# A two-layer hybrid decoder trunk on one core: state space input moved to another queue in longer pieces, and the end of the mixers reordered

## Chip, core and metric

The kernel runs on one core of one Trainium2 chip. The metric is the device time of one execution in microseconds (us), and times of several runs are given as their median. The engines are called as the profile calls them: PE is TensorE's matmul, PEld its weight load, DVE is VectorE, ACT is ScalarE, POOL is GpSimd, and SP is SyncE, which only starts transfers here.

## What is computed

Two decoder layers over 256 tokens of width 1024, all in float32. Each layer multiplies its input by one wide matrix, feeds three token mixers (an RWKV-7 time mix, multi-head latent attention, and a diagonal state space model called S5), gates and sums their outputs, normalizes, and ends with a SwiGLU network:

```python
for l in range(DEPTH):                       # DEPTH = 2
    p = x @ w_in[l]
    y_a = rwkv7_time_mix(p[..., :o_mla], ...)
    y_b = mla_branch(p[..., o_mla:o_s5], cos, sin, ...)
    y_c = s5_branch(p[..., o_s5:o_gate], ...)
    gates = sigmoid(p[..., o_gate:].reshape(bsz, t, 3, D_MODEL) + gate_b[l])
    merged = gates[..., 0, :] * y_a + gates[..., 1, :] * y_b + gates[..., 2, :] * y_c
    x = layer_norm(ALPHA * x + merged @ w_out[l], ln1_g[l], ln1_b[l])
    h = silu(x @ ffn_w1[l]) * (x @ ffn_w3[l])
    x = layer_norm(ALPHA * x + h @ ffn_w2[l], ln2_g[l], ln2_b[l])
```

## The kernel before

**Weights.** All large weights lie in DRAM as a list of 512 KB tiles (128 partitions by 1024 floats) in the order of use, 138 to a layer. For each tile SP starts one load into one of three `raw` buffers (line 160), ACT casts it to the high part `whi` (line 161), and DVE, in part POOL, computes the low part `wlo` as the remainder (lines 171 and 173). The high and low parts have four buffers each. A product with a weight is three matmuls: high by high, high by low, low by high (lines 206 to 208); a tile takes 24 of them, 8 on each line. `w_next` (line 194) hands out the next tile and, before that, lists loads until four tiles are queued, so a load that another function lists directly falls three tiles behind the tile in hand.

**Order of the work.** `ORDER1` and `ORDER2` list the units of a layer, and the loops over them (line 1283 for the second) call one function for a token. Each engine works its own instructions strictly in its order, and that order is fixed when the program is built: it follows the list, but a later unit's instructions are placed into a gap where an earlier one is expected to wait. So the units that need nothing but weights fill PE while the mixers' long chains run. In `ORDER2` these fillers are `h` (two tiles, a gate of the time mix), `o` (three tiles: a gate and the output product of the attention) and `l` (two tiles, S5's output). `v1` is the last solve of the time mix, `n1` and `y1` are the two halves of its group norm, `f0` to `f3` are its output products (one tile each, `branch0`, line 1274), which need `y1`'s result.

**Early weights.** `X` (`free`, line 1262) closes the buffers of the mixers and opens a pool on their place; `E0` to `E3` (`ffn_early`, `w_early`, line 175) each load a tile of the feed forward network through a `raw` buffer and cast it to `eh` and `el` in that pool. So the cast waits until the last instruction of `y1` is done, and the `raw` buffer is held from the load until then.

**State space input.** `s5_in` (line 692) copies the projected input out of PSUM to `u` on ACT (line 113 by way of `cp`), and eight transfers of 64 KB spread it over partitions into `U2` (line 702): SP starts them in layer 0, POOL in layer 1. Each is 32 partitions by four pieces of 512 bytes. `s5_tile` (line 724) multiplies `U2` by the tables (line 733). The profile shows these tensors as `u` and `U`.

**End of the mixers.** `norm` (line 1101) takes the square (ACT), the sum and the scale (DVE, with a power on POOL, line 240), and in its second half transposes `yT` on PE (line 1116). `out_half` (line 834) ends each output product with two DVE operations (lines 841 and 842), and the first of them frees its PSUM buffer. There are three `mm` buffers of PSUM. `token_major` (line 497) is the product with `w_out`: the first four row tiles are taken as they come, for both halves of the tokens, then four rows together; its accumulators are the three `mm` buffers and one more, and its rows 2i and 2i+1 are what `f`i wrote.

Of the kernel before, what the change touches and what calls it, by code (L numbers as in the profile page):

```python
# [19 lines left out]
NF = 22  # L20
# [9 lines left out]
ORDER2 = [  # L30
    "U K Q p0 V a0 b0 s0 a1 b1 p1 s1 i0 G0 a2 p2 l1 s2 p3 a3 l0 j0 v0 n0 s3 l2 b2 b3 l3 o3 i1 j1 v1 y0 C n1 h0 y1 h3 o1 h2 o0 X h1 f3 o2 E0 E1 E2 f0 E3 f1 f2",
    "U K Q p0 V a0 s0 a1 b0 p1 s1 i0 p2 l0 a2 b1 s2 l2 p3 b2 j0 v0 a3 s3 i1 n0 y0 l1 b3 j1 l3 v1 C h0 n1 y1 o3 X o2 E0 o0 o1 h2 E1 f0 h1 f1 h3 f3 f2 E2 E3",
]
# [40 lines left out]

PART = {"b": "a", "y": "n", "j": "i", "w": "t", "K": "U", "Q": "U", "V": "U"}


# [9 lines left out]
def trunk(ctx: ExitStack, tc: tile.TileContext, xT, xtok, ws, spA, spB, spC, sp5, lnv, cst, out, dbg=None,  # L87
# [113 lines left out]
    def inst(i):  # L201
        return getattr(i, "ins", i)

    def mm3(ps, w, x, first, last):
        (wh, wl), (xh, xl) = w, x
        PE.matmul(ps, lhsT=wh, rhs=xh, start=first, stop=False)  # L206
        PE.matmul(ps, lhsT=wh, rhs=xl, start=False, stop=False)  # L207
        PE.matmul(ps, lhsT=wl, rhs=xh, start=False, stop=last)  # L208

# [286 lines left out]

    def token_major(a, nk, ln, last, q, l, at):

        nonlocal x_dram
        lg = q.tile([128, D], F32, tag="lg", name="lg")  # L500
        lb = q.tile([128, D], F32, tag="lb", name="lb")
# [3 lines left out]
        def run(w, k, b, ns=(0, 1)):  # L505
            t = slice(128 * b, 128 * b + 128)
            for n in ns:
                s = slice(512 * n, 512 * n + 512)
                ah, al = a[0][:, k, t], a[1][:, k, t]
                PE.matmul(acc[b][n], lhsT=ah, rhs=w[0][:, s], start=(k == 0), stop=False)  # L510
                PE.matmul(acc[b][n], lhsT=ah, rhs=w[1][:, s], start=False, stop=False)  # L511
                PE.matmul(acc[b][n], lhsT=al, rhs=w[0][:, s], start=False, stop=(k == nk - 1))  # L512
# [36 lines left out]
    for l in range(layers):  # L549
# [138 lines left out]
        with tc.tile_pool(name=f"s5p{l}", bufs=1, side=P) as q:  # L688
            u = q.tile([128, 4, 2, 128], F32, tag="u", name="u")
            U2 = q.tile([128, 8, 128], F32, tag="U2", name="U2")  # L690

            def s5_in(fp):
                mark("s5proj")
                ps = proj_pair(X)
                for i in range(2):
                    cp(5, out=u[:, 2 * fp:2 * fp + 2, i, :], in_=ps.rearrange("p (f c i) -> p f i c", f=2, i=2)[:, :, i, :])
                if fp == 0:
                    return
                for j in range(4):
                    for i in range(2):  # L700
                        r = 64 * (j % 2) + 32 * i
                        (G if l else SY).dma_start(out=U2[r:r + 32, j // 2::2, :], in_=u[32 * j:32 * j + 32, :, i, :])

# [20 lines left out]
            def s5_tile(F):  # L724
# [4 lines left out]
                for pp in range(2):  # L729
                    ps = mxps("a")  # L730
                    for qq in range(2):
                        for ri in range(2):
                            PE.matmul(ps[:, 256 * qq + 128 * ri:256 * qq + 128 * ri + 128],  # L733
                                      lhsT=bl[64 * pp:64 * pp + 64, 2 * F + qq, ri, :],
                                      rhs=U2[64 * pp:64 * pp + 64, 2 * F + qq, :], start=True, stop=True)
                    ps4 = ps.rearrange("p (q r t) -> p q r t", q=2, r=2)
# [26 lines left out]
                for j in range(4):  # L763
                    qq, pp = j // 2, j % 2
                    r = slice(64 * pp, 64 * pp + 32)
                    PE.matmul(ps[32 * j:32 * j + 32, 0:128], lhsT=k0[r, 2 * F + qq, :], rhs=U2[r, 2 * F + qq, :],
                              start=True, stop=False, skip_group_check=True)
                for par in range(2):
                    for i, (ci, which, ri) in enumerate(((0, 0, 0), (0, 1, 1), (1, 1, 0), (1, 0, 1))):
                        for j in range(4):  # L770
# [6 lines left out]
                            else:  # L777
                                PE.matmul(ps[32 * j:32 * j + 32, 128:256], lhsT=lt, rhs=src, start=(i == 0),
                                          stop=(i == 3), skip_group_check=True)
                V.scalar_tensor_tensor(out=yc5[:, F, :].rearrange("p (c i) -> p i c", i=2), in0=u[:, F], scalar=A("d", F),  # L780
                                       in1=v2(ps[:, 0:256], 2), op0=ALU.mult, op1=ALU.add)
# [66 lines left out]
        if True:  # L848
# [252 lines left out]
            def norm(g):  # L1101
# [12 lines left out]
                ps = mxps("c")  # L1114
                for i in range(4):
                    PE.transpose(ps[:, 256 * (i % 2) + 128 * (i // 2):256 * (i % 2) + 128 * (i // 2) + 128],
                                 yT[:, 2 * i:2 * i + 2].rearrange("p h n -> p (h n)"), ident)
                yc = t1("BK", (128, 512))
# [170 lines left out]
        with tc.tile_pool(name=f"mg{l}", bufs=1, side=P) as q:  # L1289
            mark("wout")  # L1290
            token_major(gate0[1], 8, 0, False, q, l, [])
        gstack.close()
# [4 lines left out]
        with tc.tile_pool(name=f"ff{l}", bufs=1, side=O) as q:  # L1297
# [54 lines left out]
            with tc.tile_pool(name=f"mh{l}", bufs=1, side=P) as q2:  # L1352
                token_major((hh, hl), NF, 2, l == layers - 1, q2, l, [9, 10, 11, 12])

# [42 lines left out]
def _pack(inp):  # L1397
# [25 lines left out]
    for l in range(nl):  # L1423
# [30 lines left out]
        ws += [piece[t] for t in (ORDER1[l] + " " + ORDER2[l]).split() if t in piece]  # L1454
        ws.append(rows(g["w_out"][l]))
        w1, w3 = g["ffn_w1"][l], g["ffn_w3"][l]
# [71 lines left out]
```

## Time and profile before

| | us |
|---|---|
| median of 3 runs | 1059.97 (1058.11 to 1062.94) |
| the profiled execution | 1062.76 |
| its span, first to last instruction | 1061.0 |
| PE busy | 1012.5 (95%) |
| DVE busy | 785.4 (74%) |
| ACT busy | 485.4 (46%) |
| POOL busy | 238.8 (23%) |
| mean granted TensorE clock | 0.976 of full speed |

PE is busy nearly all of the span, so its idle stretches are short and can be listed one by one. The granted clock has two levels, 1.2 and 2.4 GHz, which the profile writes as 0.5 and 1.0. Times inside the trace are counted from the span's start.

### The profile page before, as it was taken

The page shows a single profiled execution, that of the slowest core. Times are in us where ns is not written, and L with a number is a line of the kernel's source. Part 1 is how long each engine was busy: PE and PEld are TensorE (multiplying, and loading weights), DVE is VectorE, ACT ScalarE, POOL GpSimd, SP SyncE. Part 2 cuts the span into 40 slices and gives each one's busy share as a digit, 9 for nine tenths or more (in the row PEclk, how much of TensorE's full clock was granted, in tenths as well). Part 3 has the DMA queues.
Part 4 walks back from the last instruction along what each step waited for, and adds up shares of the span by engine and source line. Part 5 has one row for each costly group of instructions (what it writes and reads, how often), then busy time and mean ns, then how long its engine had stood idle before and what let it go on. Part 6 is the DMA issues. An engine that isn't in the chain of part 4 may idle for free.

```text
span 1061.0 us, 21306 instructions
## 1 busy us (share of the span) xinstructions
PE 1012.5 (95%) x8584; PEld 910.9 (86%) x8584; DVE 785.4 (74%) x1546; ACT 485.4 (46%) x813; POOL 238.8 (23%) x270
## 2 busy tenths in 40 slices
PE   8799799999999999999998999999998899999997
PEld 7799688887897999998788989788888779999885
DVE  7969988976578778874474898898846776766546
ACT  5554467544343344443344336865343424444431
POOL 2980032200000599500022103121002420000000
PEclk9989889999999999999997999999999999999998
DMA  8543141231475655557645325223234745555572
GB/s 282 156 160 120 60 145 45 81 121 61 162 266 160 212 184 168 171 191 269 202 141 157 101 80 196 94 80 101 85 116 149 249 152 172 189 183 179 182 274 80
DMA packets 46787, 163.87 MB, mean 154 GB/s; under 512 B 5728, under 2 KB 7264, under 8 KB 46048
## 3 DMA queue, kind: packets, MB, share of 16 engines
q1 hardware_dynamic: 46144, 161.46, 46.1%
q8 instruction: 67, 1.10, 0.4%
q0 software_dynamic: 256, 0.52, 0.2%
q10 hardware_dynamic: 288, 0.52, 0.1%
q14 instruction: 32, 0.26, 0.1%
HBM read 156.72 MB, written 4.19 MB: 152 GB/s over the span
## 4 chain that ended last, share of the span: by engine, by line
PE 71%; DVE 15%; DMA 6%; ACT 4%; issue 2%; POOL 1%; SPq 0%; DVEq 0%; ACTq 0%; POOLq 0%
PE mm L208 14%; PE mm L206 14%; PE mm L207 14%; DMA raw<-in_ws 5%; PE mm L511 3%; PE mm L512 3%; PE mm L510 3%; DVE wlo L171 2%; ACT whi L161 2%; DVE z L752 2%; PE pa L960 1%; PE pa L733 1%; PE pa L1210 1%; PE pc L511 1%; PE pc L512 1%
## 5 line engine op out<-in xcount | busy, mean ns | idle before, releaser
L171 DVE TENSOR_TENSOR wlo<-raw,whi 128x1024 fp32r<-128x1024 f32 (+2 forms) x265 | 331.6, 1256 | 171.2 <-ACT whi L161 162.7
L161 ACT CAST whi<-raw 128x1024 fp32r<-128x1024 f32 (+2 forms) x267 | 277.6, 1043 | 366.3 <-PE mm L207 227.0
L206 PE MATMUL mm<-xh,whi 128*128 128x256 f32 x1312 | 378.4, 288 | 7.6 <-ACT whi L161 7.1
L208 PE MATMUL mm<-xh,wlo 128*128 128x256 f32 x1312 | 376.5, 287 | 2.5 <-DVE wlo L171 2.3
L207 PE MATMUL mm<-xl,whi 128*128 128x256 f32 x1312 | 376.3, 287 | 0.4 <-DVE xl L262 0.4
L206 PEld LDWEIGHTS mm<-xh,whi 128*128 128x128 f32 x1312 | 250.2, 191 | 13.0 <-ACT whi L161 7.5
L208 PEld LDWEIGHTS mm<-xh,wlo 128*128 128x128 f32 x1312 | 250.8, 191 | 5.8 <-DVE wlo L171 3.3
L207 PEld LDWEIGHTS mm<-xl,whi 128*128 128x128 f32 x1312 | 250.8, 191 | 3.5 <-issue 1.2
L240 POOL TENSOR_TENSOR rs<-rs,mhalf 128x1 f32<-128x1 f32 x8 | 7.8, 971 | 329.8 <-DVE rs L238 329.8
L206 PE MATMUL mm<-yh,whi 128*128 128x256 f32 x256 | 74.6, 291 | 0.3 <-ACT yh L113 0.2
L207 PE MATMUL mm<-yl,whi 128*128 128x256 f32 x256 | 74.1, 289 | 0.0
L208 PE MATMUL mm<-yh,wlo 128*128 128x256 f32 x256 | 74.0, 289 | 0.0
L511 PE MATMUL mm<-wlo,hh 128*128 128x512 f32 x132 | 52.0, 394 | 0.0
L510 PE MATMUL mm<-whi,hh 128*128 128x512 f32 x132 | 51.6, 394 | 0.0
L512 PE MATMUL mm<-whi,hl 128*128 128x512 f32 x132 | 51.5, 393 | 0.0
L206 PEld LDWEIGHTS mm<-yh,whi 128*128 128x128 f32 x256 | 48.5, 190 | 2.2 <-ACT qa L113 0.9
L208 PEld LDWEIGHTS mm<-yh,wlo 128*128 128x128 f32 x256 | 48.5, 190 | 2.0 <-issue 1.4
L207 PEld LDWEIGHTS mm<-yl,whi 128*128 128x128 f32 x256 | 48.5, 190 | 1.2 <-issue 0.6
L173 POOL TENSOR_TENSOR wlo<-raw,whi 128x384 fp32r<-128x384 f32 (+2 forms) x24 | 27.6, 1153 | 85.3 <-ACT whi L161 84.8
L967 POOL TENSOR_SCALAR_AFFINE_SELECT Mk<-Mk 64x512 f32<-64x512 f32 x32 | 26.5, 829 | 46.3 <-ACT Mk L113 45.0
L511 PEld LDWEIGHTS mm<-wlo,hh 128*128 128x128 f32 x132 | 24.8, 188 | 6.0 <-DVE wlo L171 0.6
L510 PEld LDWEIGHTS mm<-whi,hh 128*128 128x128 f32 x132 | 24.8, 188 | 5.9 <-DVE th L1306 0.5
(492 smaller groups left out, 1731.2 us busy)
## 6 DMA issues: line engine op xcount, KB each, us to landing
raw<-in_ws SPq DMA_DIRECT2D x267, 512.0 KB, 3.5
raw<-in_ws SPq DMA_DIRECT2D x8, 416.0 KB, 3.5
xd<-xk SPq DMA_DIRECT2D x3, 1024.0 KB, 5.7
lg<-in_lnv SPq DMA_DIRECT2D x4, 512.0 KB, 4.8
lb<-in_lnv SPq DMA_DIRECT2D x4, 512.0 KB, 5.2
xk<-xd SPq DMA_DIRECT2D x4, 512.0 KB, 5.2
pc<-in_spC SPq DMA_DIRECT2D x2, 768.0 KB, 5.3
pb<-in_spB SPq DMA_DIRECT2D x2, 512.0 KB, 5.1
```

Of the source, the lines that this page charges most:

```text
L161: S.copy(out=hi[:, s], in_=raw[:, s])
L171: V.tensor_tensor(out=lo[:, 0:m], in0=raw[:, 0:m], in1=hi[:, 0:m].bitcast(F32), op=ALU.subtract)
L173: G.tensor_tensor(out=lo[:, m:w], in0=raw[:, m:w], in1=hi[:, m:w].bitcast(F32), op=ALU.subtract)
L206: PE.matmul(ps, lhsT=wh, rhs=xh, start=first, stop=False)
L207: PE.matmul(ps, lhsT=wh, rhs=xl, start=False, stop=False)
L208: PE.matmul(ps, lhsT=wl, rhs=xh, start=False, stop=last)
L510: PE.matmul(acc[b][n], lhsT=ah, rhs=w[0][:, s], start=(k == 0), stop=False)
L511: PE.matmul(acc[b][n], lhsT=ah, rhs=w[1][:, s], start=False, stop=False)
L512: PE.matmul(acc[b][n], lhsT=al, rhs=w[0][:, s], start=False, stop=(k == nk - 1))
L733: PE.matmul(ps[:, 256 * qq + 128 * ri:256 * qq + 128 * ri + 128], lhsT=bl[64 * pp:64 * pp + 64, 2 * F + qq, ri, :], rhs=U2[64 * pp:64 * pp ...
L752: V.tensor_tensor_scan(out=z[:, pp, qq, ri], data0=bc(m2[:, j:j + 1], [128, 128]), data1=z[:, pp, qq, ri], initial=0.0, op0=ALU.mult, op1= ...
L967: G.affine_select(out=Mk[r, h], in_=Mk[r, h], pattern=[[0, 4], [1, 2], [1, 64]], compare_op=ALU.is_ge, fill=0.0, base=-1, channel_multipli ...
```

## The change

The state space input changes its layout so that each partition's share of a transfer is one piece of 2 KB, and ACT starts the eight transfers in both layers. The transposes of the group norm get an order edge: they may not stand before the last product of three (line 208) that was listed ahead of them. `ORDER2` is changed: in layer 0 `h3` is listed ahead of `y1`; in layer 1 the end is rewritten. The rows of `w_out` are packed and used in the order of the `f` units, so that the rows of the last `f` come last.

```diff
 ORDER2 = [
-    "... y0 C n1 h0 y1 h3 o1 h2 o0 X h1 f3 o2 E0 E1 E2 f0 E3 f1 f2",
-    "... l3 v1 C h0 n1 y1 o3 X o2 E0 o0 o1 h2 E1 f0 h1 f1 h3 f3 f2 E2 E3",
+    "... y0 C n1 h0 h3 y1 o1 h2 o0 X h1 f3 o2 E0 E1 E2 f0 E3 f1 f2",
+    "... l3 v1 C n1 h0 o3 y1 X E0 o0 E1 h3 f3 E2 f0 o2 h2 E3 f2 o1 h1 f1",
 ]
+def wout_rows(l):
+    return [k for t in ORDER2[l].split() if t[0] == "f" for k in (2 * int(t[1]), 2 * int(t[1]) + 1)]
...
+    def behind():
+
+        return tc.issue_after(inst(state["mm"]))
+
     def mm3(ps, w, x, first, last):
...
-        PE.matmul(ps, lhsT=wl, rhs=xh, start=False, stop=last)
+        state["mm"] = PE.matmul(ps, lhsT=wl, rhs=xh, start=False, stop=last)
...
-    def token_major(a, nk, ln, last, q, l, at):
+    def token_major(a, rows, ln, last, q, l, at):
...
-                ah, al = a[0][:, k, t], a[1][:, k, t]
+                ah, al = a[0][:, rows[k], t], a[1][:, rows[k], t]
...
-            u = q.tile([128, 4, 2, 128], F32, tag="u", name="u")
-            U2 = q.tile([128, 8, 128], F32, tag="U2", name="U2")
+            u = q.tile([128, 2, 4, 128], F32, tag="u", name="u")
+            U2 = q.tile([128, 2, 4, 128], F32, tag="U2", name="U2")
...
-                        (G if l else SY).dma_start(out=U2[r:r + 32, j // 2::2, :], in_=u[32 * j:32 * j + 32, :, i, :])
+                        S.dma_start(out=U2[r:r + 32, j // 2], in_=u[32 * j:32 * j + 32, i])
...
-                for i in range(4):
-                    PE.transpose(ps[:, 256 * (i % 2) + 128 * (i // 2):256 * (i % 2) + 128 * (i // 2) + 128],
-                                 yT[:, 2 * i:2 * i + 2].rearrange("p h n -> p (h n)"), ident)
+                with behind():
+                    for i in range(4):
+                        PE.transpose(ps[:, 256 * (i % 2) + 128 * (i // 2):256 * (i % 2) + 128 * (i // 2) + 128],
+                                     yT[:, 2 * i:2 * i + 2].rearrange("p h n -> p (h n)"), ident)
...
-            token_major(gate0[1], 8, 0, False, q, l, [])
+            token_major(gate0[1], wout_rows(l), 0, False, q, l, [])
...
-        ws.append(rows(g["w_out"][l]))
+        ws.append(rows(g["w_out"][l])[wout_rows(l)])
```

The operations on the copies of `u` and on `U2` index the new layout and are otherwise the same. The packing of the weight list follows `ORDER2`.

## Rows read from the trace of the kernel before

**Rows 1.** The page, busy time of each engine over the span.

```profile
PE 1012.5 (95%) x8584; PEld 910.9 (86%) x8584; DVE 785.4 (74%) x1546; ACT 485.4 (46%) x813; POOL 238.8 (23%) x270
```

**Rows 2.** PE's waits: what it waited for, us in total, times, longest us.

```profile
PE mm L206 <- ACT whi L161: 7.1, 2, 5.6
PE pc L1116 <- DVE yT L1111: 4.8, 2, 3.1
```

**Rows 3.** Timelines, layer 1's state space input: start, us, instruction [idle before <- releaser].

```profile
563.81 0.64 ACT L113 COPY u<-mm 128x256 f32<-128x256 f32 x2
564.49 4.58 POOL L702 DMA_DIRECT2D U<-u  x8 [5.11 <-ACT u L113]
565.23 1.05 ACT L161 CAST whi<-raw 128x1024 fp32r<-128x1024 f32 x1 [0.78 <-DMA raw<-in_ws]
...
571.13 2.15 PE L733 MATMUL pa<-U,bl 64*128 64x128 f32 x8 [3.77 <-DMA U<-u]
573.21 0.58 PE L206 MATMUL mm<-xh,whi 128*128 128x256 f32 x1
```

**Rows 4.** Transfers of the page: queue, count, KB each, median us from issue to landing.

```profile
U<-u SPq DMA_DIRECT2D x8, 64.0 KB, 3.0
...
U<-u POOLq DMA_DIRECT2D x8, 64.0 KB, 5.8
```

**Rows 5.** Issue of a transfer: line 702 (ns min/median/max), and ACT's timeline at the start.

```profile
L702 SPq DMA_DIRECT2D U<-u x8: 585/600/1354, 33.5 to 38.8; - x8
...
0.81 0.89 ACTq L251 DMA_DIRECT2D xr<-in_xT  x2
```

**Rows 6.** Windows: stretch, us, busy us (count) of PE, PEld, DVE, ACT, POOL, then PEclk.

```profile
48.30:58.60 10.30, 6.34 (x28) 6.04 (x29) 6.49 (x6) 6.23 (x11) 10.22 (x8) 0.50 0.36 112
...
570.60:584.20 13.60, 12.99 (x53) 11.82 (x54) 6.21 (x13) 1.56 (x2) 0.00 (x0) 0.50 0.28 71
...
806.10:809.50 3.40, 3.20 (x15) 3.21 (x16) 1.75 (x4) 0.00 (x0) 0.00 (x0) 0.50 0.40 135
...
840.20:843.60 3.40, 3.09 (x7) 2.48 (x8) 3.40 (x5) 1.74 (x2) 0.00 (x0) 0.50 0.77 242
```

**Rows 7.** Timelines of ACT and PE, layer 0's first stage.

```profile
48.76 1.33 ACT L418 ACTIVATE cd<-pb,c 128x512 f32<-128x512 f32 x2 [4.86 <-DVE pb L408]
50.00 0.45 ACT L600 ACTIVATE kr__236<-mm,dv 128x256 f32<-128x256 f32 x1
50.36 1.03 ACT L161 CAST whi<-raw 128x1024 fp32r<-128x1024 f32 x1
...
51.45 0.58 PE L206 MATMUL mm<-xh,whi 128*128 128x256 f32 x1 [5.62 <-ACT whi L161]
```

**Rows 8.** Windows with line 208 alone, layer 1: us, PE busy (count), PEld busy (count), PEclk.

```profile
767.50:811.30 43.80, 18.73 (x62) 12.04 (x61) 0.96 0.35 116
811.30:834.40 23.10, 18.08 (x65) 12.06 (x65) 1.00 0.77 259
```

**Rows 9.** Weight loads of 759 to 812.9, `whi` casts of 768 to 812.9, ACT's next casts.

```profile
L160 SPq DMA_DIRECT2D raw<-in_ws x11: 327/328/328, 759.4 to 807.0; - x11
...
L161 ACT CAST whi<-raw x9: 1041/1047/1048, 768.9 to 812.3; 128x1024 fp32r<-128x1024 f32 x9
...
813.23 1.99 ACT L161 CAST eh<-raw 128x1024 fp32r<-128x1024 f32 x2
```

**Rows 10.** Timelines of DVE and PE around the group norm, layer 1 and layer 0.

```profile
797.55 0.69 DVE L1096 TENSOR_REDUCE ssm<-pb 128x8 f32<-128x512 f32 x1 [0.94 <-PE pb L1092]
...
806.30 1.11 PE L1116 MATMUL pc<-c,yT 128*128 128x128 f32 x4 [3.13 <-DVE yT L1111]
...
812.26 0.69 DVE L1129 TENSOR_TENSOR yl<-BK,yh 128x512 fp32r<-128x512 f32 x1
...
281.12 0.66 PE L1116 MATMUL pc<-c,yT 128*128 128x128 f32 x4 [1.63 <-DVE yT L1111]
```

**Rows 11.** Timelines of ACT, DVE and PE at the start of layer 1's `w_out`.

```profile
836.55 1.04 ACT L161 CAST whi<-raw 128x1024 fp32r<-128x1024 f32 x1 [2.01 <-DMA raw<-in_ws]
...
839.78 0.68 DVE L841 SCALAR_TENSOR_TENSOR gate<-gate,mm 128x512 f32<-128x512 f32 x1
...
840.51 0.80 PE L510 MATMUL mm<-whi,msh 128*128 128x512 f32 x1 [4.23 <-DVE gate L841]
```

More of the change, by code (lines that the diff above doesn't have):

```diff
@@ L30 @@
 ORDER2 = [
-    "U K Q p0 V a0 b0 s0 a1 b1 p1 s1 i0 G0 a2 p2 l1 s2 p3 a3 l0 j0 v0 n0 s3 l2 b2 b3 l3 o3 i1 j1 v1 y0 C n1 h0 y1 h3 o1 h2 o0 X h1 f3 o2 E0 E1 E2 f0 E3 f1 f2",
-    "U K Q p0 V a0 s0 a1 b0 p1 s1 i0 p2 l0 a2 b1 s2 l2 p3 b2 j0 v0 a3 s3 i1 n0 y0 l1 b3 j1 l3 v1 C h0 n1 y1 o3 X o2 E0 o0 o1 h2 E1 f0 h1 f1 h3 f3 f2 E2 E3",
+    "U K Q p0 V a0 b0 s0 a1 b1 p1 s1 i0 G0 a2 p2 l1 s2 p3 a3 l0 j0 v0 n0 s3 l2 b2 b3 l3 o3 i1 j1 v1 y0 C n1 h0 h3 y1 o1 h2 o0 X h1 f3 o2 E0 E1 E2 f0 E3 f1 f2",
+    "U K Q p0 V a0 s0 a1 b0 p1 s1 i0 p2 l0 a2 b1 s2 l2 p3 b2 j0 v0 a3 s3 i1 n0 y0 l1 b3 j1 l3 v1 C n1 h0 o3 y1 X E0 o0 E1 h3 f3 E2 f0 o2 h2 E3 f2 o1 h1 f1",
 ]
@@ L495, in layer_norm @@
         yield
-    def token_major(a, nk, ln, last, q, l, at):
+    def token_major(a, rows, ln, last, q, l, at):
         nonlocal x_dram
+        nk = len(rows)
         lg = q.tile([128, D], F32, tag="lg", name="lg")
@@ L695, in s5_in @@
                 for i in range(2):
-                    cp(5, out=u[:, 2 * fp:2 * fp + 2, i, :], in_=ps.rearrange("p (f c i) -> p f i c", f=2, i=2)[:, :, i, :])
+                    cp(5, out=u[:, i, 2 * fp:2 * fp + 2, :], in_=ps.rearrange("p (f c i) -> p f i c", f=2, i=2)[:, :, i, :])
                 if fp == 0:
@@ L734, in s5_tile @@
                                       lhsT=bl[64 * pp:64 * pp + 64, 2 * F + qq, ri, :],
-                                      rhs=U2[64 * pp:64 * pp + 64, 2 * F + qq, :], start=True, stop=True)
+                                      rhs=U2[64 * pp:64 * pp + 64, qq, F, :], start=True, stop=True)
                     ps4 = ps.rearrange("p (q r t) -> p q r t", q=2, r=2)
@@ L765, in s5_tile @@
                     r = slice(64 * pp, 64 * pp + 32)
-                    PE.matmul(ps[32 * j:32 * j + 32, 0:128], lhsT=k0[r, 2 * F + qq, :], rhs=U2[r, 2 * F + qq, :],
+                    PE.matmul(ps[32 * j:32 * j + 32, 0:128], lhsT=k0[r, 2 * F + qq, :], rhs=U2[r, qq, F, :],
                               start=True, stop=False, skip_group_check=True)
@@ L779, in s5_tile @@
                                           stop=(i == 3), skip_group_check=True)
-                V.scalar_tensor_tensor(out=yc5[:, F, :].rearrange("p (c i) -> p i c", i=2), in0=u[:, F], scalar=A("d", F),
+                V.scalar_tensor_tensor(out=yc5[:, F, :].rearrange("p (c i) -> p i c", i=2), in0=u[:, :, F], scalar=A("d", F),
                                        in1=v2(ps[:, 0:256], 2), op0=ALU.mult, op1=ALU.add)
@@ L1352, in trunk @@
             with tc.tile_pool(name=f"mh{l}", bufs=1, side=P) as q2:
-                token_major((hh, hl), NF, 2, l == layers - 1, q2, l, [9, 10, 11, 12])
+                token_major((hh, hl), range(NF), 2, l == layers - 1, q2, l, [9, 10, 11, 12])
 def _constants():
```

## The prediction

> **What bounds the kernel now.** I read the page first: PE is busy 95% of the span [rows 1], so only PE's idle time and stretches at half clock can be won. Next came the waits of PE, to see which of its idle stretches the change touches [rows 2], then the timelines around each of them, and last the granted clock. Four stalls matter here. In layer 1 PE waits 3.8 us for the state space input [rows 3], and the next 13.6 us run at 0.50 of the clock [rows 6]. In layer 0 PE waits 5.6 us for a cast [rows 7], with 10.3 us at 0.50 around it [rows 6]. The norm's transposes wait 1.6 us in layer 0 and 3.1 us in layer 1 [rows 10]. Layer 1's `w_out` waits 4.2 us [rows 11]. After the last two 3.4 us run at half clock each [rows 6]. A stretch at half clock costs half its length where PE is full.
>
> **Part 1, the state space input of layer 1.** ACT finishes `u` at 564.45; POOL then starts eight transfers in 4.58 us, and PE's first product waits until 571.13 [rows 3]. That product needs only the first two of the eight (blocks of 32 columns, `j` = 0). The new transfers need a price for an issue on ACT and for a landing. An issue on ACT took 0.89/2 = 0.45 us for 128 pieces of 2 KB, one on SP 0.60 us for the same 64 KB in 512 byte pieces [rows 5]. With 32 pieces I take 0.40 us, near ACT's own row; ends are 0.35 and 0.65. Landing took 3.0 us from SP and 5.8 us from POOL [rows 4]; I take 3.0, since ACT's queue, like SP's, has no software behind it, and keep 5.8 as the other end. The second transfer is then issued at 564.9 and lands at 567.9 instead of 571.0. PE was ready for it at 567.1, where its preceding matmul stood, so the stall falls from 3.8 to about 0.8 us: 3.1 us won.
>
> The clock: each of the gaps of 3.1 us and more in rows 7, 10, 11 and 3 was followed or accompanied by half clock, the gap of 1.6 us in layer 0 was not [rows 6, 10]. With a gap of 0.8 us I expect the 13.6 us at full clock: 6.8 us won. Sum of part 1: **-9.9 us**.
>
> What stands behind the issues on ACT: eight times 0.40 is 3.2 us, so the cast at 565.23 [rows 3] moves to about 567.7, its low part to 570. Its first product stood at 573.21 and can now be wanted at about 569; 0.5 us may be lost there and is inside my rounding. SP's queue is not touched in layer 1; POOL's 4.58 us had no other work behind it.
>
> **Part 1 in layer 0.** `U` is not wanted there until PE reaches it at 75 us, so landing is free. SP is freed of eight issues of 0.60 us, behind which weight loads stood. But ACT gets 3.2 us of issues at 33.6, ahead of casts and of the table copies (line 418) for which DVE's in-place products wait. That chain ends in the copies at 48.76, behind which the cast at 50.36 stands that PE waits for [rows 7]. Part of the 3.2 us falls into ACT's idle time; I charge **+1.5 us**. Bounds: +6.3, if an issue costs 0.65 (5.2 us: 3.1 on that chain, 1.5 on the cast before it, 1.7 for one more half clock stretch of 3.4 us), and -9, if the new order places that cast ahead of the copies (5.6 idle and 3.5 of clock).
>
> **Part 2, the transposes.** The order edge holds them behind the last product listed before them: `h3`'s in layer 0, `o3`'s in layer 1. In both layers PE had finished that unit long before (it stood in `o0` at 281 and in `h2` at 806), so the edge moves nothing: **0**. Both gaps stay unless the order moves for another reason.
>
> **Part 3, layer 1's new order.** First what it wins: E2 and E3 leave the end. Before, the first DVE step that frees the last PSUM buffer ran at 839.78, behind a low part whose cast waited for its load until 836.55, and PE waited for it [rows 11]. With the loads spread, that wait and its clock go: 4.2 + 0.5 x 3.4 = 5.9 us, and the rows of the last `f` now come last.
>
> Then what it costs. From 767.5 to 811.3, while the last inverse, solve and norm run, PE executed 62 matmuls of line 208, 7.75 tiles of filler [rows 8]. After it eight tiles remained, in 23.1 us, 2.85 us each. The new list puts `f3` and `f0`, which need the norm, ahead of `o2`, `h2` and `o1`, and E0, E1, E2 before them too. An early weight holds its `raw` buffer until the norm is over: of eleven loads from 759.4 to 807.0 nine were cast to `whi`, and the other two came out as `eh` only at 813.23, right behind the norm's last instruction, 812.26 + 0.69 [rows 9, 10]. The load of an early weight falls three tiles behind its place, so E0 comes after `o0`, E1 after `f3`, E2 after the second tile of `o2`. There all three `raw` buffers are held and no weight can be loaded. Filler from 767.5 is then `h3` and two tiles of `o2`, four instead of 7.75. PE runs out near 788, and twelve tiles, not eight, remain after the norm: 4 x 2.85 = 11.4 us more behind it.
>
> What gives it back: ACT and DVE have no casts then, so the chain runs alone. From the sum at 797.55 to the norm's end the chain took 15.4 us [rows 10]; its own instructions, added up, are about 10.5, and some 2 us more come off the solve. The norm ends about 6.9 us earlier, at 804.4. Then 804.4 + 12 x 2.85 + 1.0 (refilling the three buffers) + 1.7 (one half clock stretch after the idle time) = 841.3, against 811.3 + 23.1 + 0.4 (the gap ahead of the first six) + 5.9 = 840.7. So **+1 us**. Bounds: +8, if the chain gains nothing, and -5.9, if filler does not run out. Layer 0's list only swaps `h3` and `y1`, whose weights keep their order, and its `w_out` gaps wait for weights, not rows: 0.
>
> **Sum.** -9.9 + 1.5 + 1.0 = -7.4 us. The profiled execution took 1062.8, so 1055.4 on its own count; it lies 2.8 above the median of 1060.0, and against that the forecast is **1052.6 us**. About 0.5%, 5.3 us, is what a measurement can tell from no change.
>
> **Rivals.**
> 1. Filler does not run out (the loads of E1 and E2 are placed later than the list says). For it: PE was nearly full before; against it: rows 9. Then -9.9 + 1.5 - 5.9 = -14.3, 1045.7. If the transposes' gaps went too (1.6 + 3.1 + 1.7), 1039.
> 2. The input lands no sooner. Layer 1's transfers run beside weight loads, and if these, not POOL, made 5.8 us of 3.0, the second lands at 570.7 and the stall and the half clock stay: -0.4 + 1.5 + 1.0, 1062.1, no change. Against it: SP's eight ran beside loads as well [rows 4]. The Trainium skill, page DMA: Bandwidth & Descriptors, section Issuing engines are not separate DMA queues, says that transfers of all issuing engines share the same 16 DMA engines and that another queue saves only issue time. By that rule this rival holds; rows 4 speak against it, though their two layers differ in load.
> 3. Slower: ACT's queue is held. Place: between the copy of `u` and the casts. Price: 0.65 us an issue, SP's row [rows 5], 5.2 us each time: +6.3 in layer 0; in layer 1 the first product behind moves only from 573.2 to 572, -1.2; with +1 at the end +6.1, 1066.1. It decides from about 0.55 us an issue.
> 4. Filler runs out and the chain gains nothing: -9.9 + 1.5 + 8 = -0.4, 1059.6, no change.
>
> **How the numbers follow.** Forecast 0.37 (its own range 1048 to 1057; 0.27 of it below 1054.7), rival 1 0.20, rival 2 0.18, rival 3 0.13, rival 4 0.12. Faster by over 0.5%: 0.27 + 0.20 + 0.01 = 0.48. Slower by over 0.5%: 0.08 of rival 3, 0.05 of rivals 2 and 4, 0.01 of the rest: 0.14. The rest, 0.38, is no change. The range reaches from below rival 1 to rival 3, leaving out the lowest end of the one and the upper of the other: 1042 to 1067.
>
> **What would show it.** In the changed trace: eight issues on ACT behind layer 1's copy of `u` at 0.40 us each, PE's wait for `U` near 0.8 us, and full clock after it. Layer 0's wait of 5.6 us about 1.5 longer. The transposes' waits still there. PE with sparse work for some 15 us before layer 1's `f3`, the casts to `eh` right after the norm, and no wait of 4 us in `w_out`. A wait for `U` of 3 us or more, an issue over 0.55 us, or filler up to the norm's end would prove the sum wrong.

## The result, and the profile after

The changed kernel is slower: 1071.68 us (median, 1069.59 to 1072.88) against 1062.21 us for the kernel before in the same runs, a ratio of 1.0079 with a 95% interval of 1.0055 to 1.0103. By the ratio 8.4 us are lost (the medians lie 9.5 us apart), where 7.4 us less was forecast. The profiled execution took 1071.48 us, its span is 1069.8 us. One execution each of `layout_only`, `e2later` and `sp_efill` below took 1.03 to 2.9 times as long as the others of its kernel and is left out of all medians and ratios.

Where the time went is seen when the span is cut at points that both programs pass: in each layer the first product of the feed forward network with a weight tile of the running list (it stands right behind the products with E0 to E3), and in layer 1 the last products of `r0` (the unit just ahead of the first state space tile), of `G0` (the last gate unit) and of `o3`. The times are read from PE's timeline of each trace.

| us | before | after | difference |
|---|---|---|---|
| start to layer 0's feed forward network | 354.8 | 361.2 | +6.4 |
| from there to layer 1's `r0` | 211.4 | 211.6 | +0.2 |
| `r0` to `G0`, with the state space input | 92.5 | 90.7 | -1.8 |
| `G0` to `o3` | 101.4 | 102.0 | +0.6 |
| `o3` to layer 1's feed forward network | 117.1 | 120.5 | +3.4 |
| the rest | 183.8 | 183.7 | -0.1 |

Three stages hold all of it: layer 0's first half lost 6.4 us, the input of layer 1 won 1.8, layer 1's end lost 3.4. The same cuts of the traces below show how far one execution can be trusted. Thirteen profiles of kernels that start the input on SP in layer 0 gave 354.8 to 357.5 for the first stage, 356.6 on average, so the trace of before was a lucky one there and +4.6 is the fairer figure. Eight with the input on POOL in layer 1 and the list ahead of it unchanged gave 88.2 to 93.2, on average 91.5, for the third, so that only 0.8 of the 1.8 us stand against the average, well inside that spread. Eight with the old order gave 114.0 to 117.9, on average 116.0, for the end, against which the changed kernel lost 4.5.

The page's first part and PE's waits after the change, to hold against [rows 1] and [rows 2]:

```profile
PE 1017.6 (95%) x8584; PEld 915.4 (86%) x8584; DVE 786.1 (73%) x1546; ACT 485.9 (45%) x813; POOL 234.2 (22%) x262
```

```profile
PE mm L217 <- DVE wlo L176: 6.8, 4, 5.3
...
PE pc L1127 <- DVE yT L1121: 4.6, 2, 3.0
PE pa L743 <- DMA U<-u: 4.1, 2, 3.1
```

The wait of 5.6 us for a cast has only changed its name (now 5.3 us for a low part), the transposes still wait as in [rows 10], and the wait for the input has grown from 3.8 to 4.1 us. The wait of 4.2 us in `w_out` [rows 11] is gone from the list.

**Layer 0.** Timelines of ACT, DVE and PE after the change (start, us, instruction, idle before and releaser):

```profile
32.86 0.64 ACT L118 COPY u<-mm 128x256 f32<-128x256 f32 x2
33.26 6.33 ACTq L712 DMA_DIRECT2D U<-u  x8
39.63 1.99 ACT L166 CAST whi<-raw 128x1024 fp32r<-128x1024 f32 x2 [6.13 <-DMA U<-u]
...
40.71 3.70 DVE L176 TENSOR_TENSOR wlo<-raw,whi 128x1024 fp32r<-128x1024 f32 x2 [4.97 <-ACT whi L166]
...
55.31 0.58 PE L217 MATMUL mm<-xh,wlo 128*128 128x256 f32 x1 [5.29 <-DVE wlo L176]
```

Eight issues hold ACT for 6.33 us. The casts behind them start at 39.63; in the kernel before one stood at 33.65 and one at 36.59, as its ACT timeline shows:

```profile
33.65 1.05 ACT L161 CAST whi<-raw 128x1024 fp32r<-128x1024 f32 x1
...
36.59 1.05 ACT L161 CAST whi<-raw 128x1024 fp32r<-128x1024 f32 x1
```

DVE, which makes their low parts, idles for 4.97 us and then still has the in-place products of the tables to do. PE feels it at 55.31.

**The input of layer 1.** Timelines of ACT and PE, and windows (stretch, us, busy us and count of PE, PEld, DVE, ACT, POOL, then PEclk):

```profile
571.06 5.18 ACTq L712 DMA_DIRECT2D U<-u  x8
...
577.07 0.68 PE L743 MATMUL pa<-U,bl 64*128 64x128 f32 x4 [3.14 <-DMA U<-u]
578.67 1.19 PE L743 MATMUL pa<-U,bl 64*128 64x128 f32 x4 [0.92 <-DMA U<-u]
```

```profile
578.60:585.40 6.80, 6.73 (x25) 5.69 (x25) 2.82 (x4) 1.95 (x4) 0.00 (x0) 0.50 0.07 12
585.40:592.00 6.60, 6.60 (x56) 6.54 (x56) 5.99 (x11) 3.47 (x6) 0.00 (x0) 1.00 0.46 150
```

PE was ready some 3 us after the first issue and waited twice, 4.1 us together. The stretch at half clock behind it is 6.8 us instead of 13.6 [rows 6], worth some 3.4 us where PE is full: what the stage won comes from there, not from an earlier landing. The shorter stretch can't be put down to the change. With the input on POOL it was 6.8 us in the profile of `e_late` below and 13.7 in that of `order_only`, and with the input on ACT in layer 1 alone (`act_l1`) it was 13.7.

**Layer 1's end.** DVE's and ACT's timelines at the end of the norm, SP's timeline, then windows of the products' last line (line 217, formerly 208: us, PE busy with its count, PEld, PEclk), to hold against [rows 8] and [rows 9]:

```profile
807.79 0.69 DVE L1140 TENSOR_TENSOR yl<-BK,yh 128x512 fp32r<-128x512 f32 x1
...
808.67 2.94 ACT L166 CAST eh<-raw 128x1024 fp32r<-128x1024 f32 x3 [7.98 <-DVE yl L1140]
...
750.08 44.53 SPq L165 DMA_DIRECT2D raw<-in_ws  x8
808.58 0.33 SPq L529 DMA_DIRECT2D lg<-in_lnv  x1
808.96 0.43 SPq L529 DMA_DIRECT2D lb<-in_lnv  x1
811.00 3.75 SPq L165 DMA_DIRECT2D raw<-in_ws  x3
```

```profile
773.00:808.50 35.50, 9.89 (x34) 6.22 (x33) 0.93 0.20 68
808.50:850.00 41.50, 28.34 (x92) 19.76 (x92) 0.85 0.74 248
```

The norm ends at 808.5, and right behind it three tiles are cast to `eh` at once: E0, E1 and E2 had filled all three `raw` buffers. SP started its last load at about 794 and the next at 811.0. In the 35.5 us ahead of the norm's end PE had 34 matmuls of the line, 4.25 tiles; behind it are 92, 11.5 tiles, in 41.5 us.

The clock around the norm's end, in windows of all engines as above:

```profile
803.90:814.10 10.20, 8.33 (x32) 7.24 (x33) 6.17 (x9) 2.94 (x3) 0.00 (x0) 0.50 0.45 143
...
817.50:824.30 6.80, 6.04 (x26) 5.75 (x27) 4.63 (x7) 3.10 (x4) 0.00 (x0) 0.50 0.86 296
```

### The profile page after: what moved, and what is told of

It reads as the page before. It is cut to its first block, busy times and chain, and to the rows that moved or that the text cites. A ratio compares the mean times of both kernels' runs of the same rounds, so it can differ in the third digit from the quotient of the medians.

```text
span 1069.8 us, 21295 instructions
## 1 busy us (share of the span) xinstructions
PE 1017.6 (95%) x8584; PEld 915.4 (86%) x8584; DVE 786.1 (73%) x1546; ACT 485.9 (45%) x813; POOL 234.2 (22%) x262
## 4 chain that ended last, share of the span: by engine, by line
PE 70%; DVE 15%; DMA 6%; ACT 5%; issue 2%; POOL 1%; ACTq 1%; DVEq 0%; SPq 0%; POOLq 0%
PE mm L215 14%; PE mm L217 14%; PE mm L216 14%; DMA raw<-in_ws 5%; PE mm L520 3%; PE mm L521 3%; PE mm L522 3%; DVE wlo L176 3%; ACT whi L166 2%; PE pa L970 1%; DVE z L762 1%; PE pa L1221 1%; PE pc L522 1%; PE pc L520 1%; PE pc L521 1%
## 5 line engine op out<-in xcount | busy, mean ns | idle before, releaser
L215 PE MATMUL mm<-yh,whi 128*128 128x256 f32 x256 | 77.0, 302 | 4.1 <-ACT whi L166 2.5
L217 PE MATMUL mm<-yh,wlo 128*128 128x256 f32 x256 | 76.4, 298 | 0.5 <-DVE wlo L176 0.5
L216 PE MATMUL mm<-yl,whi 128*128 128x256 f32 x256 | 76.4, 298 | 0.0
L215 PEld LDWEIGHTS mm<-yh,whi 128*128 128x128 f32 x256 | 50.9, 199 | 6.7 <-ACT whi L166 2.7
L217 PEld LDWEIGHTS mm<-yh,wlo 128*128 128x128 f32 x256 | 50.9, 199 | 2.7 <-issue 1.4
L216 PEld LDWEIGHTS mm<-yl,whi 128*128 128x128 f32 x256 | 51.0, 199 | 1.3 <-issue 0.6
L249 POOL TENSOR_TENSOR rsn<-rsn,mhalf 128x8 f32<-128x8 f32 x4 | 6.6, 1638 | 128.4 <-DVE rsn L247 128.4
```

The costliest lines, as they stand in the source:

```text
L217: state["mm"] = PE.matmul(ps, lhsT=wl, rhs=xh, start=False, stop=last)
L249: G.tensor_tensor(out=out, in0=in_, in1=mh(out), op=ALU.pow)
```

## Experiments

Each ratio is that of the kernel's runs to those of the kernel before on the same chip, with its 95% interval. The stages are cut as above, in each kernel's own profile.

### Which part costs what

`u_only`: the kernel before with the state space input's part of the change alone.

```diff
-                        (G if l else SY).dma_start(out=U2[r:r + 32, j // 2::2, :], in_=u[32 * j:32 * j + 32, :, i, :])
+                        S.dma_start(out=U2[r:r + 32, j // 2], in_=u[32 * j:32 * j + 32, i])
```

> The kernel before with the state space input's part of the change alone (2 KB pieces, ACT's queue in both layers). Theory A (the input's move costs some 5 us: ACT is held 6.3 us in layer 0, and in layer 1 the landing is no shorter): 5 to 6 us slower than before, 1065 to 1068, layer 0's time up to the last output unit 6 us longer, layer 1's wait for the input about 3 us. Rival B (the slowdown comes from the new order, the input's part is won as predicted or even): 1050 to 1062.

`order_only`: the changed kernel with the line above and the layout of `u` and `U2` put back.

> The changed kernel with the state space input put back on its old queues and in its old pieces: what is left is the order, the transposes' edge and the rows of w_out. Theory A: 3 to 4 us slower than before, 1065 to 1067, with no row of layer 0 moved by more than 0.5 us; PE starved ahead of the norm's end in layer 1 and no wait in w_out. Rival B: as slow as the changed kernel, 9 us over before.

`layout_only`: the new layout, the old queues.

```diff
+                        (G if l else SY).dma_start(out=U2[r:r + 32, j // 2], in_=u[32 * j:32 * j + 32, i])
```

> The kernel before with the new pieces of 2 KB but the old queues (SP in layer 0, POOL in layer 1). Theory A (the queue, not the pieces, makes the loss, and landing is set by the traffic beside it): within 2 us of before, 1060 to 1064, layer 1's landing 5 to 6 us as before. Rival C (512 byte pieces made the old landing long): landing in layer 1 near 4 us, wait 1 to 2 us shorter, half-clock stretch gone, 1052 to 1057.

`act_l1`: the same with `(S if l else SY)`.

> The kernel before with the new pieces, SP in layer 0 as before and ACT's queue in layer 1 alone. Theory A (layer 0's hold is the loss): 1 us faster to even, 1059 to 1062; issues of 0.6 us on ACT, landing 4.5 to 5.5 us, wait about 3 us. Rival B (layer 1's hold on ACT costs as well): 3 to 5 us slower than before.

| | median us | ratio | start to layer 0's network | `r0` to `G0` | `o3` to the network |
|---|---|---|---|---|---|
| u_only | 1066.38 | 1.0029 (1.0007 to 1.0050) | 360.8 | 89.1 | 114.0 |
| order_only | 1066.34 | 1.0036 (1.0023 to 1.0048) | 356.5 | 91.4 | 120.9 |
| layout_only | 1062.66 | 1.0000 (0.9983 to 1.0017) | 356.6 | 91.7 | 115.4 |
| act_l1 | 1062.61 | 0.9986 (0.9967 to 1.0005) | 357.5 | 92.9 | 117.9 |

Both parts lose, and their losses add: 0.29 + 0.36 is 0.65 of the 0.79%, the difference lying inside the intervals. Each stands in its own stages: the input's part leaves the end alone, the order leaves layer 0 alone. The 2 KB pieces by themselves change nothing that can be told from zero (0.17% either way). On ACT in layer 1 alone the input wins at most 0.33% by the interval, and none of it can be told from zero. `u_only` came out below what theory A gave it, 3.1 us and not 5 to 6; in its profile, taken of one of its faster executions (1062.03 us), layer 0 lost 4.2 us against the average, and the stage from `r0` won 2.4.

### The price of an issue on ACT

`act16`: each of the eight transfers cut in two.

```diff
-                        S.dma_start(out=U2[r:r + 32, j // 2], in_=u[32 * j:32 * j + 32, i])
+                        for h in range(0, 32, 16):
+                            S.dma_start(out=U2[r + h:r + h + 16, j // 2], in_=u[32 * j + h:32 * j + h + 16, i])
```

> The kernel with the input's part alone, each of the eight transfers cut in two by partitions: 16 transfers of 16 pieces of 2 KB. Theory A (each issue on ACT has a fixed price of about 0.6 us, and ACT's queue stands for it): the hold in layer 0 doubles to some 10 to 12 us, and the kernel is 4 to 7 us slower than with eight, 1070 to 1074. Rival D (the price goes by pieces, so the sum of pieces sets the hold): 16 issues of 0.3 us, the same 1066.

`act_late`: in layer 0 the eight are listed behind the gate unit `G1`.

```diff
+            def gate2(fp):
+                gate_pair(2, fp, M[:, 2 * fp:2 * fp + 2])
+                if l == 0 and fp == 1:
+                    u_out()
```

> The kernel with the input's part alone, but in layer 0 the eight issues on ACT are listed behind the second gate unit (G1) instead of right behind the copy of u; the planner may spread them. Theory A (the loss in layer 0 is the eight issues in one block ahead of two casts and the tables' copies): 4 to 6 us faster than eight in one block, 1060 to 1062, no wait over 3 us before 60 us. Rival E (ACT's time for the issues costs wherever it stands): still 1065 or more.

The line of the issues in layer 0, of the changed kernel, of `act16` and of `act_late` (ns min, median, max; first and last start):

```profile
L712 ACTq DMA_DIRECT2D U<-u x8: 594/602/1861, 33.3 to 39.0; - x8
```

```profile
L703 ACTq DMA_DIRECT2D U<-u x16: 600/600/1171, 33.7 to 43.9; - x16
```

```profile
L706 ACTq DMA_DIRECT2D U<-u x8: 514/515/612, 35.3 to 58.3; - x8
```

In a row an issue takes 0.60 us whether it moves 32 pieces or 16, and one started each 0.64 us or so; by itself, in `act_late`, it takes 0.51. `act16` is 1.0104 (1.0082 to 1.0126), 1075.40 us; against `u_only` the first stage grew from 360.8 to 366.4 and `r0` to `G0` from 89.1 to 94.3, 5.6 and 5.2 us for eight more issues in each, 0.65 to 0.70 an issue. The runs give less: the two ratios differ by 0.75%, about 8 us for sixteen issues, 0.5 each, and theirs is the safer figure, since `u_only`'s profile was a fast one. Either way most of the price of an issue in one block goes through to the end. `act_late` is 0.9972 (0.9949 to 0.9995), 1061.61 us, and its first stage takes 355.9: the loss of layer 0 is gone, with the same eight issues on the same engine. ACT's timeline of `act_late` shows why:

```profile
48.97 1.04 ACT L161 CAST whi<-raw 128x1024 fp32r<-128x1024 f32 x1
49.79 0.52 ACTq L706 DMA_DIRECT2D U<-u  x1
49.91 0.47 ACT L600 ACTIVATE kr__236<-mm,dv 128x256 f32<-128x256 f32 x1
```

The issue starts while the cast still runs and lasts until 50.31, and the next instruction starts at 49.91, about when the cast ends. A single issue between two others is hidden; of the changed kernel's eight in a row, 6.33 us long, ACT waited 6.13. One part of what was expected of `act_late` did not come: PE has a wait of 4.62 us for ACT at 59.80.

### The wait for the input, and what sets the landing

`t0_late` takes most of the wait away without touching the transfers: in layer 1's first list `t0`, the first state space tile, moves behind `r1`.

```diff
-    "m S0 S1 P r0 N t0 r1 k r2 t1 ...",
+    "m S0 S1 P r0 N r1 t0 k r2 t1 ...",
```

> The kernel before, with one token of layer 1's first list moved: the first state space tile (t0) stands behind r1 instead of ahead of it, so that PE has two tiles of weight work while the input is on its way. It prices the wait and the half clock behind it, whatever queue brings the input. If the forecast's price for them was right (3 us of wait and 6.8 us of clock), 8 to 10 us faster, 1053 to 1055. If most of the stage is bound by something else, 0 to 3 us, 1060 to 1063.

`sp_both` is `layout_only` with `SY.dma_start` in both layers.

> The kernel before with the new pieces and all transfers of the input started by SP, in layer 1 too. Theory A (landing beside weight loads is set by the loads in flight, whatever engine issues): in layer 1 transfers issued while two or three loads are in flight land after 4 to 7 us, the wait of PE is 3 us or more, time 1061 to 1068. Rival H (SP's transfers land in 3 us as in layer 0 because of the queue): landing 3 us, wait under 1.5 us, 1054 to 1059.

`t0_late` is 0.9932 (0.9907 to 0.9957), 1057.82 us: what it takes of the wait and its clock is worth 7.2 us with an interval of 4.6 to 9.9. Its profile, of a slower execution (1060.01 us), shows less: a wait of 1.41 us, 3.4 us at half clock behind it, and 88.1 us from `r0` to `G0`, 3.4 under the average. `sp_both` is 0.9937 (0.9914 to 0.9960), 1056.35 us; its figures are those of rival H, 4.7 us under the least that theory A gave it. SP's timeline of the kernel before, then SP's and PE's of `sp_both`, with its windows behind the input:

```profile
560.70 8.56 SPq L160 DMA_DIRECT2D raw<-in_ws  x5
```

```profile
561.46 3.60 SPq L160 DMA_DIRECT2D raw<-in_ws  x3
566.30 5.00 SPq L702 DMA_DIRECT2D U<-u  x8
571.40 7.77 SPq L160 DMA_DIRECT2D raw<-in_ws  x4
...
570.57 1.04 PE L733 MATMUL pa<-U,bl 64*128 64x128 f32 x8 [1.09 <-DMA U<-u]
```

```profile
570.00:575.00 5.00, 4.43 (x31) 3.83 (x32) 3.51 (x6) 4.11 (x9) 0.00 (x0) 1.00 0.65 211
575.00:584.00 9.00, 9.00 (x76) 8.84 (x75) 8.05 (x18) 4.20 (x7) 0.00 (x0) 1.00 0.54 182
```

In the kernel before SP starts five weight loads of 512 KB from 560.7 to 569.3, so three of them go out with the input. In `sp_both` the input stands in SP's own queue, and no load starts from 565.1 to 571.4. The time from issue to landing in layer 1 (min, median, max), of the kernel before (POOL), the changed kernel (ACT), `sp_both` (SP) and `act16` (ACT, 32 KB each):

```profile
DMA to landing us min/median/max: 3.5/5.8/7.0
```

```profile
DMA to landing us min/median/max: 3.8/5.0/5.8
```

```profile
DMA to landing us min/median/max: 2.0/2.4/3.9
```

```profile
DMA to landing us min/median/max: 2.0/2.0/3.7
```

So ACT's transfers land in 2.0 us as well when the loads have stopped (in `act16` ACT is held so long that SP has no free buffer to load into), SP's took up to 4.1 us in layer 0 of the kernel before beside loads, and one of POOL's, in `order_only`, took 2.4; rival H's reason, a shorter way by SP's queue, is not needed for them. What differs is how many weight loads are in flight; this is read from these traces, and a kernel that only holds the loads back, with the input on ACT or POOL, was not tried.

Nor did ACT's transfers always take 5.0 us. PE's timeline and the landing in `u_only`, then PE's timeline in `act_late`, both with ACT in layer 1 as in the changed kernel:

```profile
573.89 0.68 PE L733 MATMUL pa<-U,bl 64*128 64x128 f32 x4 [0.49 <-DMA U<-u]
576.52 0.68 PE L733 MATMUL pa<-U,bl 64*128 64x128 f32 x4 [1.94 <-DMA U<-u]
...
DMA to landing us min/median/max: 2.3/3.0/4.6
```

```profile
569.20 0.68 PE L742 MATMUL pa<-U,bl 64*128 64x128 f32 x4 [0.41 <-DMA U<-u]
571.76 0.68 PE L742 MATMUL pa<-U,bl 64*128 64x128 f32 x4 [1.87 <-DMA U<-u]
```

The median landing is 3.0 us here and 3.2 in `act_late`, and PE's first wait is short. But the next four products need the third and the fourth transfer, and PE waits again. The third was issued 0.2 us behind a weight load in both, and landed with it: 4.6 us after its issue, the loads 4.4 and 4.7 after theirs. The same pair took 5.8 and 6.0 us in the changed kernel and 3.7 and 3.8 in `act16`; in `act_l1` it was 4.8 and 6.1, so this is no strict rule. In `u_only` and `act_late` 6.8 us at half clock follow, and `r0` to `G0` takes 89.1 and 89.0 us, some 2.5 under the average.

`sp_both` shows the wait at 1.1 us, the clock at 1.00 behind it, and `r0` to `G0` in 84.0 us against 91.5 on average: 7.5 us.

### Layer 1's end

Five lists, each against the old or the new one. `e_spread` is the kernel before with E2 and E3 moved, and the rows of `w_out` in the order of the `f` units; the others are `order_only` with another list.

```diff
 before:     ... o3 X o2 E0 o0 o1 h2 E1 f0 h1 f1 h3 f3 f2 E2 E3
+e_spread:   ... o3 X o2 E0 o0 o1 h2 E1 f0 E2 h1 f1 E3 h3 f3 f2
 changed:    ... o3 y1 X E0 o0 E1 h3 f3 E2 f0 o2 h2 E3 f2 o1 h1 f1
+efill:      ... o3 y1 X o0 h3 o2 h2 E0 f3 E1 f0 E2 f2 o1 E3 h1 f1
+e2later:    ... o3 y1 X E0 o0 E1 h3 f3 f0 o2 h2 E2 f2 E3 o1 h1 f1
+f_late:     ... o3 y1 X E0 o0 E1 h3 E2 o2 h2 f3 f0 E3 f2 o1 h1 f1
+e_late:     ... o3 y1 X o0 h3 f3 f0 o2 h2 E0 E1 f2 E2 o1 E3 h1 f1
```

> The kernel before with the end of layer 1's list alone changed: the early weights E2 and E3 move ahead of h1 and h3, E0, E1 and the fillers stay where they were, and the rows of w_out follow the f units. Theory A (what the new order loses is filler ahead of the norm's end, because E0, E1 and E2 hold all three raw buffers; what it wins is w_out's wait): 3 to 6 us faster, 1057 to 1060, no wait over 1 us in w_out, weight work of PE up to the norm's end as before. Rival F (moving the loads forward makes other weights late): even or slower.

> The order's part alone (the input on its old queues), with layer 1's end listed with the fillers first: X o0 h3 o2 h2 E0 f3 E1 f0 E2 f2 o1 E3 h1 f1. Theory A (E0, E1 and E2 hold the three raw buffers and starve PE of filler ahead of the norm's end): PE keeps weight work up to the norm's end (over 55 instead of some 40 matmuls of the last line of a product in the 43 us before it), 3 to 7 us faster than the order as changed, 1058 to 1062. Rival G (the loss is in w_out or in the loads after the norm): no faster than the order as changed, 1065 or more.

> The order's part alone, with the list as changed but E2 moved from ahead of f0 to behind h2, and E3 behind f2 as E2's neighbour: two early weights, not three, can stand in raw buffers before the norm's end. Theory A: the third buffer carries filler, so 1 to 4 us faster than the order as changed, 1061 to 1065. If the third buffer alone cannot carry it, or the tiles of f3 and f0 hold the cast buffers instead, the same 1066.

> The order's part alone, the early weights E0, E1, E2 placed early as in the change, but f3 and f0 moved behind the fillers: X E0 o0 E1 h3 E2 o2 h2 f3 f0 E3 f2 o1 h1 f1. If the three raw buffers held by E0 to E2 alone starve PE: no faster than the order as changed, 1065 or more. If f3 and f0, whose cast tiles hold two of the four cast buffers until the norm is over, starve it: as fast as the version with the fillers first, 1056 to 1060.

> The mirror of it: E0, E1 behind h2, E2 and E3 after f2, with f3 and f0 early as in the change: X o0 h3 f3 f0 o2 h2 E0 E1 f2 E2 o1 E3 h1 f1. If the raw buffers alone are the cause: 1056 to 1060. If the cast buffers alone are: 1065 or more. If either is enough to starve PE, both this and its mirror stay at 1064 or more.

| | median us | ratio | `o3` to the network, us | matmuls of the last line in the 40 us before the norm's end, and from it to `w_out` |
|---|---|---|---|---|
| before | | 1 | 117.1 | 58, 61 |
| e_spread | 1063.19 | 0.9991 (0.9977 to 1.0006) | 116.4 | 54, 61 |
| order_only | 1066.34 | 1.0036 (1.0023 to 1.0048) | 120.9 | 46, 92 |
| e2later | 1068.41 | 1.0048 (1.0026 to 1.0069) | 119.7 | 48, 84 |
| f_late | 1069.55 | 1.0047 (1.0029 to 1.0065) | 121.9 | 48, 88 |
| e_late | 1063.32 | 1.0000 (0.9979 to 1.0021) | 118.0 | 46, 80 |
| efill | 1058.21 | 0.9957 (0.9941 to 0.9973) | 112.9 | 59, 69 |

Windows of the last line for `efill` and `f_late`, the 40 us ahead of the norm's end and from there to `w_out`, then SP's timeline of `f_late` up to its first load behind the norm:

```profile
768.10:808.10 40.00, 16.80 (x59) 11.02 (x59) 1.00 0.35 118
808.10:832.40 24.30, 19.19 (x69) 12.83 (x69) 1.00 0.79 282
```

```profile
766.50:806.50 40.00, 13.85 (x48) 8.83 (x47) 0.94 0.17 54
806.50:848.30 41.80, 25.37 (x88) 17.19 (x88) 0.85 0.74 248
```

```profile
761.90 22.49 SPq L165 DMA_DIRECT2D raw<-in_ws  x5
806.69 0.33 SPq L529 DMA_DIRECT2D lg<-in_lnv  x1
807.07 0.43 SPq L529 DMA_DIRECT2D lb<-in_lnv  x1
809.05 2.60 SPq L165 DMA_DIRECT2D raw<-in_ws  x3
```

`efill` settles the main point: with the fillers listed ahead of the early weights, PE has 59 matmuls of the line ahead of the norm's end instead of 46, the clock stays at 1.00, and 0.36% lost becomes 0.43% won. Which buffers starve it took the other three. In `f_late` the early weights alone do it: SP starts no load for 25 us (784.4 to 809.05). In `e_late` they are gone and PE is still short ahead of the norm (46), which, by the list, is left to `f3` and `f0`, whose cast tiles hold two of the four cast buffers until the norm is over; but fewer tiles remain and they go through at full clock, 80 matmuls in 30.2 us. Its time lies between what had been expected of the one cause and of the other. By the counts either is enough to starve PE, and the early weights cost more: without them the order is even with the kernel before, and with `f3` and `f0` also moved it wins 0.43%. `e2later` was a miss: taking one early weight back frees a `raw` buffer, but `f3` and `f0` then hold two of the cast buffers, and the kernel was no faster.

`e_spread` says what the wait in `w_out` was worth by itself: it is gone, and the kernel is at most 0.23% faster, where 3 to 6 us were expected. In its place `w_out`'s tiles wait for their weights (1.09 us at 853.74), and around the norm's transposes 6.8 us ran at half clock (from 806.4) instead of 3.4 [rows 6].

### Both gains together

`t0_efill` is `efill` with `t0` behind `r1`; `sp_efill` is `efill` with the input as in `sp_both`.

> The version with the fillers first, and layer 1's first state space tile behind r1. If both gains hold and add: 8 to 12 us faster than before, 1052 to 1056 by the count of the first runs of before. If the half clock or the loads give one of them back: as the tile moved alone, about 7 us faster.

> The version with the fillers first, and all transfers of the input started by SP in 2 KB pieces. If the two gains (6.2 us of 1062.6 for SP, 4.3 us for the fillers first) add: 1051 to 1053. If SP's gain depends on where the loads stood and is lost here: 1058.

`t0_efill` is 0.9916 (0.9891 to 0.9940), 1053.77 us; `sp_efill` is 0.9903 (0.9879 to 0.9927), 1053.65 us. Both beat the kernel before, by some 9 and 10 us, and the changed one, by some 18. The gains add within the intervals: for `sp_efill` 0.63 and 0.43% alone are 1.06, together 0.97; for `t0_efill` 0.68 and 0.43 are 1.11, together 0.84.

## Why the prediction was wrong, point by point

**The issue on ACT** was the step that failed first. It was priced at 0.40 us by ACT's two issues of `xr` [rows 5]; it took 0.60, what SP's row for the same transfer said in the same group. The range had 0.65 as its upper end, and it was put down as rival 3 with a chance of 0.13. With it failed the step "part of the 3.2 us falls into ACT's idle time; I charge +1.5 us": the block was 6.33 us, and layer 0 lost 6.4 us by the traces (4.6 against the average of thirteen). The rival's place, mechanism and threshold of 0.55 were right, and its chance too low; that its +6.3 met the trace's +6.4 is in part luck, since the profile of before had the shortest first stage of the thirteen.

**The landing** was the second, and the larger by size: of 9.9 us the changed kernel got 1.8, or 0.8 against the average. "I take 3.0, since ACT's queue, like SP's, has no software behind it" was a reason from the queue; in the changed kernel the median was 5.0 us and the range 3.8 to 5.8, and PE waited 4.1 us instead of 0.8. As far as these traces show, rival 2 had it: what stands beside the transfers decides. A second step failed with it, "the stall falls from 3.8 to about 0.8 us" with full clock behind: it counted only the two transfers that the first products need. `u_only` and `act_late` had the forecast's landing (3.0 and 3.2) and its first wait (0.49 and 0.41), and still won only some 2.5 us in the stage against the average, for PE waited 1.94 and 1.87 us for the next two transfers and half clock followed. The Trainium skill, page DMA: Bandwidth & Descriptors, section Issuing engines are not separate DMA queues, says that transfers of all issuing engines run on the same 16 DMA engines and interleave, and the traces agree (medians of 5.8 us on POOL and 5.0 on ACT beside loads; 2.0 on ACT, in 32 KB pieces, and 2.4 on SP with no load started). The second half of its rule, that the time to initiate is "usually small relative to the DMA itself", does not hold here: 0.60 us to issue against 2.0 us to land, eight times in a row on an engine with casts behind it, made the loss. Nor does the rule lead to what won, the same transfers on the loads' own queue; that they are faster because the loads stand behind them there is read from the traces, as said above.

**The price of the wait** was right in kind and on the high side. It was 3.1 us of wait and 6.8 of clock, 9.9 together; `t0_late`, which takes most of both away, won 7.2 (4.6 to 9.9), and `sp_both`, with a wait of 1.1 us and full clock, 7.5 us in that stage. The 9.9 lies at the end of the interval. The changed kernel kept the wait (3.14 and 0.92 us) and had half the slow stretch, whose length differed among the other kernels with the input on the same queue.

**The transposes**: right. They wait 1.63 and 2.99 us, against 1.63 and 3.13 before [rows 10], for `yT` as before, and the changed kernel written without the edge is the very same program, so the edge moves nothing. Layer 0's swap of `h3` and `y1` moved nothing either: `order_only`, which has it, needs 356.5 us for the first stage, the average of the thirteen being 356.6.

**Layer 1's order**: the mechanism was right in each step, a size was off. Forecast were 4 tiles of filler, measured 4.25; 12 tiles behind the norm, measured 11.5; the three casts to `eh` right behind it; no wait in `w_out`, whose stretch shrank by 6.4 us, 5.9 forecast. The norm ended earlier than said: 808.5 against 813.0 with a layer that began 5.4 us later is 9.9 us, not 6.9. The term that was too small is the refilling: 1.0 us and 1.7 of clock were allowed, but from the norm's end to `w_out` it took 41.4 us for 11.5 tiles, 8.6 us above 2.85 each. PE waited 2.51 and 0.46 us for weights there, and 12.4 us of it, to 814.1 and from 817.5 to 824.3, ran at 0.50, which is some 6 us. The first weight load was started at 811.0, when DVE had made the first low part out of the early weights' `raw` buffers (from 809.75 on), and took 5.7 us to land, beside the 1 MB of `lg` and `lb` started ahead of it. The sum had a slip too: it counted the norm's end back from 811.3, where [rows 10] put it at 812.95, and with that it gives 1.6 us more. In sum +3.4 instead of +1, inside the bounds of -5.9 and +8. Whether the order of `lg` and `lb` matters was not tried.

The sum: -9.9 + 1.5 + 1.0 was forecast, -1.8 + 6.4 + 3.4 came, with 0.7 in the stages between. Two of its three signs of being wrong came, an issue over 0.55 us and a wait of over 3 us for `U`. Rivals 2 and 3 share no step and both came true, where each had been taken alone: by the prediction's own terms the two together are -0.4 + 6.3 + 1.0 = +6.9 us, just at the upper end of the range, and the end's 2.4 us above its term went past it. The rest is that the runs of before beside it had a median 2.2 us above the one shown ahead of the prediction.

## What to carry to other kernels

Price a DMA issue by the row of the same transfer, whichever engine it is on, and count the block of issues as time of that engine: a run of them behind one another stops its stream, one at a time between longer instructions cost nothing here. Count every transfer that the next products need, not the first ones alone. A small transfer that something waits for landed late beside bulk loads, whichever of three engines started it; starting it in the loads' own queue, so that the bulk stands behind it, won 0.63% here. A weight that is loaded early but can only be unpacked late holds its staging buffer all that time: list the work that is to fill the gap first, and keep at least one staging buffer and the cast buffers out of the hands of anything that waits for the gap's end.

## What was not expected of the hardware

A 64 KB transfer inside the chip's memory took 0.59 to 0.60 us to issue from SP, in 512 byte and in 2 KB pieces, 0.60 from ACT in a row and 0.51 by itself, and 0.55 and 0.50 from POOL; cut to 32 KB it still took 0.60. In layer 0 one issue of the eight took longer, 1.35 us on SP in the kernel before, 1.86 on ACT in the changed one and 2.53 in `u_only`; why stays open. The issue of a transfer on ACT runs beside the instruction in hand, so that a lone one was free (`act_late`) and a row of them was not.
